# A hybrid attention and SSM layer on one core: SSM products of two halves in turn, joined scans, SSM issued ahead of the q and k pass, and row blocks in the order 0, 1, 3, 2

## The chip, the cores and the metric

The kernel runs on one core of a Trainium2 chip. The metric is device time in microseconds of one execution of the whole program, from inputs in HBM to outputs in HBM.

## The reference, cut to what matters

One layer over 2048 prompt rows and 64 sample rows of width 1024, in fp32:

```python
proj = x @ w_in                                  # q | k | v | u, 512 columns each
attn = diff_attention(rope(q), rope(k), v)       # 8 heads, two softmax maps each, chunk-causal
y    = Re(C h) + D u                             # S5 SSM: 32 groups of 16 channels, 64 complex states
ssm  = glu(gelu(y) @ w_glu + b_glu)
x1   = layer_norm(ALPHA * x + concat(attn, ssm) @ w_out)
x2   = layer_norm(ALPHA * x1 + square(relu(x1 @ w_up)) @ w_down)    # w_up 1024 x 4096
```

The sample rows attend to a cache of 1024 keys and values (`cache_k`, `cache_v`). The outputs are x2, the new k and v rows, and the last SSM states.

## The kernel before

**Products.** Most products are written as three fp32r products (`mm3`, L136 to L138): high times high, low times high, high times low. So each weight is split into a high part on ACT (L130) and a low part on DVE or POOL (L133). The SSM products are plain fp32, and each stands in the trace as two PE instructions.

**Stages.** (1) `proj_uv` makes u and v. (2) `proj_qk` makes q and k (PSUM tile `pm`), and beside it run `ssm_all` and `cache_keys`, which splits and stores the cached keys and values. (3) `attention` over 72 units (a unit is one head by 256 rows, or the 64 sample rows of one head; its product ends in the ACT copy `osb`, L581), beside it `glu` (`za`, `zb`) and then the row blocks. (4) What is left of the blocks.

**Row blocks.** Rows go through the last two lines of the reference in four blocks, three of 512 rows and block 3 of 576. `block_out` multiplies by w_out (`pd<-dh,bxh`), adds, takes the first layer norm (LN1) and transposes back (`pu<-ident,acc`, L1058). `block_ffn` goes over 32 slices f of w_up and w_down: the up product (`pu<-bxh,fwh`), relu squared (L1167), the down product (`pd<-dh,hh`); its `rest` is the last slices and the second layer norm (LN2). `blocks()` is a generator that `interleave` advances beside attention: blocks 0, 1 and 2 in it, block 3 in the code at the end, after attention's pools are closed.

**SSM.** `ssm_build` makes the matrices of 8 groups, `ssm_run` runs them, four times over. In `ssm_run`: input products (`psi`), a rotation (`turn`), 16 scans for the four pairs of groups in real and imaginary part (prompt of 256 steps and sample of 8 apart), the rotation back, and per group g the output: one product with `km` over 128 partitions and two with `gf` over 64, the even groups in partitions 0 to 63, the odd ones in 64 to 127, all three into one PSUM tile `psy` of the pool `ps`, which has two (PSB = 2). GELU then reads `psy` (ACT, DVE, ACT, DVE) and stores to `s_gy`, from which `glu` loads `gyg`.

**What sets the order.** The work is written as Python generators, and the Tile framework gives each engine one list of instructions in order; the priority of a stretch is set with `level(n)` (n times 100000), of attention with HIP = 200000. Within an engine nothing overtakes. All loads and stores are issued by one queue, SP's (L125). `U8` is the level of the SSM's steps beside the pass, 0 before. The weights of `glu` (`wrg`) have level U7 = 3. `cache_keys` has no level and one buffer for each of its tiles (CKB = 1).

Of the kernel before, what the change touches and what calls it, by code (L numbers as in the profile page):

```python
# [45 lines left out]
ZB = 1  # L46
# [10 lines left out]
R6 = 4  # L57
R7 = 0.75
LATE = 2
# [10 lines left out]
A0S = 0  # L70
U8 = 0
VVB = 2
# [41 lines left out]
def build(nc, tc, io, ctx):  # L114
# [556 lines left out]
    def ssm_disc(kp, sp):  # L671
# [74 lines left out]
    def ssm_build(w, bt):  # L746

        ss = k.ss  # L750
        HG = SSM_HG
# [44 lines left out]
        yield  # L796
        k0 = bp.tile([128, HG, 128], F32, tag="btm", name="k0")[0:C]
        dd = bp.tile([C, HG, C], F32, tag="dd", name="dd")
        for e in range(2):
            psk = pm.tile([C, HP, 128], F32, tag="pi", name="psk", bufs=IB)  # L800
            o = slice(e * 64, e * 64 + 64)
            for q in range(HP):
                for ri in range(2):
                    pe.matmul(psk[:, q, :], lhsT=bb[o, ri, q, :], rhs=m.gf[o, ri, q, 0:8, :].rearrange("p t c -> p (t c)"),
                              start=ri == 0, stop=ri == 1)
            act.activation(out=k0.rearrange("c (q e) n -> c e q n", e=2)[:, e], in_=psk, func=AF.Copy)
        tt(dve, dd, ss.dsb[:, gs].unsqueeze(2).to_broadcast([C, HG, C]), ident[0:C, 0:C].unsqueeze(1).to_broadcast([C, HG, C]), ALU.mult)
# [9 lines left out]
        for l in range(1, 8):  # L817
# [3 lines left out]
            for ri in range(2):  # L821
                tt(pool, e[:, ri, :, n:2 * n], e[:, ri, :, 0:n], ss.u[:, 0, l, qs].unsqueeze(2).to_broadcast([128, HP, n]), ALU.mult)
                tt(pool, tmp[:, ri], e[:, 1 - ri, :, 0:n], us, ALU.mult)
                tt(pool, e[:, ri, :, n:2 * n], e[:, ri, :, n:2 * n], tmp[:, ri], (ALU.subtract, ALU.add)[ri])
        pool.tensor_copy(out=e[:, :, :, JP:NJ], in_=e[:, :, :, 0:NJ - JP])
        w.mats = m
        yield

    def ssm_run(w, m, bt):
# [39 lines left out]
        for ri in range(2):  # L869
            for q in range(HP):  # L870
                for c0, c1, i in ((0, JP, 0.0), (JP + 1, NJ, h0[:, ri, q:q + 1])):
                    dve.tensor_tensor_scan(out=z[:, ri, q, c0:c1], data0=ss.rho[:, bt * HP + q:bt * HP + q + 1].to_broadcast([128, c1 - c0]),
                                           data1=v[:, ri, q, c0:c1], initial=i, op0=ALU.mult, op1=ALU.add)
        turn(v, z, (ALU.subtract, ALU.add))
        for i, j in enumerate((JP - 1, NJ - 1)):
            pool.tensor_copy(out=ss.fin[:, i, :, qs], in_=v[:, :, :, j])
        yield
        for g in range(HG):
            psy = pm.tile([128, 512], F32, tag="ps", name="psy")
            y = psy[:, :NJ]  # L880
# [5 lines left out]
            gy = sp.tile([128, NJ], F32, tag="gy", name="gy", bufs=GB)  # L886
            act.activation(out=gy, in_=y, func=AF.Square, scale=math.sqrt(0.044715))
            dve.scalar_tensor_tensor(out=gy, in0=gy, scalar=1.0, in1=y, op0=ALU.add, op1=ALU.mult)
            act.activation(out=gy, in_=gy, func=AF.Tanh, scale=GC)
            dve.scalar_tensor_tensor(out=gy, in0=gy, scalar=1.0, in1=y, op0=ALU.add, op1=ALU.mult)  # L890
            gg = bt * HG + g
            dma(out=GY[gg * C:(gg + 1) * C, :, :].rearrange("c t j -> t c j"), in_=gy)
            if g % 4 == 3:
                yield
# [396 lines left out]
    def blocks():  # L1291
        yield from urgent(fl, U4)
        block_pools(cw, w)
        for i, b in enumerate(B):
            b.px, b.h, b.hh, b.dd, b.loaded, b.early = w.x, w.h, w.h, w.dn, False, EARLY and i == 0
# [12 lines left out]
        for i in range(3):  # L1308
            b = B[i]
            if i and not b.loaded:  # L1310
                yield from rest()
                rest = none
                while not ready(b):
                    yield "wait"
                load(b)
            state.cur = i
            yield from block_out(w, b, rest)
            if i < 2:
                rest = yield from block_ffn(w, b, lambda: load_rows(B[i + 1]), lambda: load(B[i + 1]))
            else:  # L1320
                state.rest = yield from block_ffn(w, b)

# [26 lines left out]
    with cw:  # L1349
        f2 = blocks()  # L1350
        with ExitStack() as ca:
            a = attn_pools(ca, ABUF, APB)
            hd = [None]

            def main():
                hd[0] = yield from attention_all(a)
            interleave(main(), f2, None)
            for _ in hd[0]:
                next(f2, None)
            for _ in range(R5):  # L1360
                next(f2, None)
        with ExitStack() as c2:
            p = lambda n, b, **kw: c2.enter_context(tc.tile_pool(name="o" + n, bufs=b, side="right", **kw))
            b = B[3]
            while state.cur < 2:
                next(f2)
            b.px, b.pacc, b.h = p("x", 1), p("acc", 1), p("h", HB3)
            w.ps["pu"].append(p("pu", 2, space=PSUM))
            w.ps["pd"].append(p("pd", 3, space=PSUM))
            for _ in range(R6):  # L1370
                next(f2, None)
# [6 lines left out]
            def rest():
                yield from f2
                yield from state.rest()  # L1380
            interleave(block_out(w, b, rest), f2, R7)
            w.top.close()
            with ExitStack() as c3:
                b.hold, b.lg = HL, 1
                b.hh, b.dd = (c3.enter_context(tc.tile_pool(name="t" + n, bufs=i, side="left")) for n, i in (("h", HL), ("d", 2 * HL)))

                load_gb(b, "ln2", c3.enter_context(tc.tile_pool(name="tg", bufs=1, side="left")))

                def last():
                    r = yield from block_ffn(w, b)  # L1390
                    yield from r()
                run(last())

# [65 lines left out]
```

## Time and profile before

| | us |
|---|---|
| median of 3 runs | 3173.56 (3170.77 to 3175.68) |
| profiled execution, its time | 3174.97 |
| profiled execution, its span | 3173.1 |
| PE busy | 2909.3 (92%) |
| DVE, ACT, POOL busy | 1761.8, 1504.2, 1636.2 |
| mean granted clock of PE | 0.947 of full speed |

PE is the busiest engine, but a busy PE is not PE at its peak: a matmul that streams at half clock, or that waits for its input with the next one queued, counts as busy too. So the number of matmuls in a stretch is read beside the busy time. The chain that ended last is 55% PE, 12% DVE, 11% DMA.

### The profile page before, as it was taken

The page shows a single profiled execution, that of the slowest core. Times are in us where ns is not written, and L with a number is a line of the kernel's source. Part 1 is how long each engine was busy: PE and PEld are TensorE (multiplying, and loading weights), DVE is VectorE, ACT ScalarE, POOL GpSimd, SP SyncE. Part 2 cuts the span into 40 slices and gives each one's busy share as a digit, 9 for nine tenths or more (in the row PEclk, how much of TensorE's full clock was granted, in tenths as well). Part 3 has the DMA queues.
Part 4 walks back from the last instruction along what each step waited for, and adds up shares of the span by engine and source line. Part 5 has one row for each costly group of instructions (what it writes and reads, how often), then busy time and mean ns, then how long its engine had stood idle before and what let it go on. Part 6 is the DMA issues. An engine that isn't in the chain of part 4 may idle for free.

```text
span 3173.1 us, 46490 instructions
## 1 busy us (share of the span) xinstructions
PE 2909.3 (92%) x15648; PEld 2423.9 (76%) x15648; DVE 1761.8 (56%) x4631; ACT 1504.2 (47%) x2905; POOL 1636.2 (52%) x1552
## 2 busy tenths in 40 slices
PE   8999998998898999998689999986899998899996
PEld 7976666896687888786589888864777776788885
DVE  7126866677867665567876666654222226322225
ACT  3222223776775766665567766522232322332332
POOL 2236761455654666565546666534445544544443
PEclk9999998798899999998789999998899998899998
DMA  6368875658534444446434333265223322422221
GB/s 189 128 194 212 219 204 166 202 155 276 147 107 131 130 134 119 119 118 213 144 114 129 100 110 107 76 230 179 74 83 94 89 83 80 130 80 77 80 84 56
DMA packets 420195, 425.47 MB, mean 134 GB/s; under 512 B 53458, under 2 KB 313042, under 8 KB 418932
## 3 DMA queue, kind: packets, MB, share of 16 engines
q1 hardware_dynamic: 419956, 422.50, 45.0%
q8 instruction: 123, 2.02, 0.3%
q14 instruction: 116, 0.95, 0.1%
HBM read 328.76 MB, written 93.64 MB: 133 GB/s over the span
## 4 chain that ended last, share of the span: by engine, by line
PE 55%; DVE 12%; DMA 11%; POOL 6%; issue 4%; ACT 3%; SPq 1%; POOLq 0%; DVEq 0%; ACTq 0%
PE pd L136 7%; PE pd L137 7%; PE pd L138 7%; PE pu L136 5%; PE pu L138 5%; PE pu L137 5%; DMA raw<-in_w_up 4%; PE oT L575 4%; PE tps L559 3%; PE sps L512 3%; DMA raw<-in_w_down 2%; POOL dl L133 2%; POOL fwl L133 2%; DVE acc L141 2%; DMA raw<-in_ln_g 2%
## 5 line engine op out<-in xcount | busy, mean ns | idle before, releaser
L133 POOL TENSOR_TENSOR dl<-raw,dh 128x512 fp32r<-128x512 f32 x336 | 432.8, 1301 | 294.5 <-ACT dh L130 286.3
L133 POOL TENSOR_TENSOR fwl<-raw,fwh 128x512 fp32r<-128x512 f32 x256 | 332.3, 1300 | 380.2 <-ACT fwh L130 355.3
L136 PE MATMUL pu<-bxh,fwh 128*128 128x256 f32 (+2 forms) x1472 | 496.3, 339 | 26.0 <-ACT fr L1167 17.0
L515 DVE TENSOR_SCALAR_CACHE_REDUCE s<-sps 128x512 f32<-128x512 f32 (+5 forms) x688 | 402.9, 600 | 210.9 <-PE sps L512 132.3
L141 POOL TENSOR_TENSOR s<-s 128x512 f32<-128x512 f32 (+3 forms) x344 | 382.6, 1139 | 237.4 <-ACT s L543 237.0
L138 PE MATMUL pu<-bxh,fwl 128*128 128x256 f32 (+2 forms) x1472 | 491.4, 337 | 7.0 <-POOL fwl L133 6.1
L137 PE MATMUL pu<-bxl,fwh 128*128 128x256 f32 (+2 forms) x1472 | 490.6, 334 | 0.0
L136 PE MATMUL pd<-dh,hh 128*128 128x512 f32 (+1 forms) x1088 | 426.5, 400 | 18.6 <-DVE acc L141 10.1
L137 PE MATMUL pd<-dl,hh 128*128 128x512 f32 (+1 forms) x1088 | 430.8, 396 | 0.7 <-POOL dl L133 0.7
L141 DVE TENSOR_TENSOR acc<-acc,pd 128x512 f32<-128x512 f32 (+1 forms) x384 | 254.3, 682 | 302.1 <-PE pd L138 300.8
L523 ACT ACTIVATE s<-s,nm 128x1024 f32<-128x1024 f32 (+9 forms) x416 | 365.8, 881 | 116.7 <-DVE nm L520 113.0
L138 PE MATMUL pd<-dh,hl 128*128 128x512 f32 (+1 forms) x1088 | 419.5, 396 | 0.0
L130 ACT ACTIVATE dh<-raw 128x512 fp32r<-128x512 f32 x336 | 209.2, 628 | 353.8 <-PE pd L138 209.1
L130 ACT ACTIVATE fwh<-raw 128x512 fp32r<-128x512 f32 x256 | 160.5, 628 | 378.9 <-DMA raw<-in_w_up 243.0
L136 PEld LDWEIGHTS pu<-bxh,fwh 128*128 128x128 f32 x1472 | 283.7, 193 | 68.9 <-ACT fr L1167 28.5
L132 DVE CAST hh<-fr 128x256 fp32r<-128x256 f32 (+2 forms) x184 | 111.2, 604 | 397.3 <-ACT fr L1168 397.0
L138 PEld LDWEIGHTS pu<-bxh,fwl 128*128 128x128 f32 x1472 | 282.2, 193 | 40.7 <-POOL fwl L133 15.3
L137 PEld LDWEIGHTS pu<-bxl,fwh 128*128 128x128 f32 x1472 | 283.8, 193 | 26.4
L575 PE MATMUL oT<-w,vt 128*128 128x256 f32 (+3 forms) x1296 | 258.2, 301 | 18.2 <-DVE w L133 12.8
L136 PEld LDWEIGHTS pd<-dh,hh 128*128 128x128 f32 (+1 forms) x1088 | 202.0, 186 | 63.1 <-DVE acc L141 12.0
L575 PEld LDWEIGHTS oT<-w,vt 128*128 128x128 f32 (+1 forms) x1296 | 211.3, 202 | 48.1 <-DVE w L133 20.4
L512 PE MATMUL sps<-kst,qst 96*128 96x512 f32 (+2 forms) x544 | 218.6, 419 | 20.9 <-DVE s L515 18.5
(273 smaller groups left out, 5890.0 us busy)
## 6 DMA issues: line engine op xcount, KB each, us to landing
raw<-in_w_up SPq DMA_DIRECT2D x256, 256.0 KB
raw<-in_w_down SPq DMA_DIRECT2D x256, 256.0 KB
kst<-s_k SPq DMA_DIRECT2D x64, 384.0 KB
raw<-in_w_out SPq DMA_DIRECT2D x80, 256.0 KB
xr<-in_xT SPq DMA_DIRECT2D x64, 256.0 KB
vt<-s_v SPq DMA_DIRECT2D x32, 512.0 KB
qst<-s_q SPq DMA_DIRECT2D x64, 192.0 KB
raw<-in_ln_g SPq DMA_DIRECT2D x36, 256.0 KB
```

Source lines behind the costliest of these rows:

```text
L130: act.activation(out=dst_hi, in_=src, func=AF.Copy)
L132: hi_eng.tensor_copy(out=dst_hi, in_=src)
L133: (lo_eng or dve).tensor_tensor(out=dst_lo, in0=src, in1=dst_hi.bitcast(F32), op=ALU.subtract)
L136: pe.matmul(ps, lhsT=lh, rhs=rh, start=start, stop=False)
L137: pe.matmul(ps, lhsT=lh, rhs=rl, start=False, stop=False)
L138: pe.matmul(ps, lhsT=ll, rhs=rh, start=False, stop=stop)
L141: e.tensor_tensor(out=out, in0=a, in1=b, op=op)
L512: pe.matmul(ps[:nr, :e - c0], lhsT=qst[m][0:96, q], rhs=self.keys(m, 96, c0, e), start=True, stop=True)
L515: dve.tensor_scalar(out=s[:nr, o:o + c1 - c0], in0=ps[:nr, :c1 - c0], scalar1=1.0, scalar2=None, op0=ALU.mult, op1=ALU.max, accum_out=self ...
L523: act.activation(out=x, in_=x, func=AF.Exp, bias=nm, accum_out=self.ls[:nr, m, p:p + 1])
L559: pe.transpose(out=ps[:kr, i * nr:i * nr + nr], in_=self.s[t, 0, k_ * 128 // SC][:nr, o:o + kr], identity=ident[:nr, :nr])
L575: pe.matmul(self.oT[:, t * nr:(t + n) * nr], lhsT=vt[k_ // 8][:kr, k_ % 8, :], rhs=w[:kr, e, i * nr:(i + n) * nr], start=(k_ == 0 and e == ...
```

## The change

The SSM part: the `gf` products of an even and an odd group stand in turn, each of the pair with its own `psy` tile; the scans of one part are joined into one over 1060 steps, with a decay tile `rh` that holds zeros where a segment starts; the input products' copies are all on ACT; the products for `km` (`psk`) are done for both halves at once with a tile `bz` that holds `bb` in two blocks and zeros; and U8 = 1. The block part: `blocks()` ends with block 1; block 3 follows (`block_out` beside what is left of `f2`), then its FFN with block 2's `block_out` beside it, then block 2's FFN with block 3's `rest` beside it; both have their w_out weights in a pool of their own (`wo`).

```diff
-R7 = 0.75
+R7 = 1.0
+R8 = 0.4
-U8 = 0
+U8 = 1
...
+        m.rh = w.kp.tile([128, HP, NJ + 1], F32, tag="rh", name="rh", bufs=EB)
...
+        bz = bp.tile([128, 2, HP, 2, C], F32, tag="bz", name="bz")
+        pool.memset(bz, 0.0)
         for e in range(2):
-            psk = pm.tile([C, HP, 128], F32, tag="pi", name="psk", bufs=IB)
             o = slice(e * 64, e * 64 + 64)
-            for q in range(HP):
-                for ri in range(2):
-                    pe.matmul(psk[:, q, :], lhsT=bb[o, ri, q, :], rhs=m.gf[o, ri, q, 0:8, :].rearrange("p t c -> p (t c)"),
-                              start=ri == 0, stop=ri == 1)
+            pool.tensor_copy(out=bz[o, :, :, e, :], in_=bb[o])
+        psk = pm.tile([2 * C, HP, 128], F32, tag="pi", name="psk", bufs=IB)
+        for q in range(HP):
+            for ri in range(2):
+                pe.matmul(psk[:, q, :], lhsT=bz[:, ri, q].rearrange("p e c -> p (e c)"), rhs=m.gf[:, ri, q, 0:8, :].rearrange("p t c -> p (t c)"),
+                          start=ri == 0, stop=ri == 1)
...
+        pool.tensor_copy(out=m.rh, in_=ss.rho[:, qs].unsqueeze(2).to_broadcast([128, HP, NJ + 1]))
+        pool.memset(m.rh[:, :, 0:JP + 2:JP + 1], 0.0)
...
-                if ri == 0:
-                    act.activation(out=z[:, ri, q, :], in_=psi[:, :NJ], func=AF.Copy)
-                else:
-                    dve.tensor_copy(out=z[:, ri, q, :], in_=psi[:, :NJ])
+                act.activation(out=z[:, ri, q, :], in_=psi[:, :NJ], func=AF.Copy)
...
         for ri in range(2):
-            for q in range(HP):
-                for c0, c1, i in ((0, JP, 0.0), (JP + 1, NJ, h0[:, ri, q:q + 1])):
-                    dve.tensor_tensor_scan(out=z[:, ri, q, c0:c1], data0=ss.rho[:, bt * HP + q:bt * HP + q + 1].to_broadcast([128, c1 - c0]),
-                                           data1=v[:, ri, q, c0:c1], initial=i, op0=ALU.mult, op1=ALU.add)
+            dve.tensor_tensor_scan(out=zt[:, ri].rearrange("p q j -> p (q j)"), data0=m.rh.rearrange("p q j -> p (q j)"),
+                                   data1=vt[:, ri].rearrange("p q j -> p (q j)"), initial=0.0, op0=ALU.mult, op1=ALU.add)
...
-        for g in range(HG):
-            psy = pm.tile([128, 512], F32, tag="ps", name="psy")
-            y = psy[:, :NJ]
-            o = slice(g % 2 * 64, g % 2 * 64 + 64)
-            pe.matmul(y, lhsT=m.km[:, g, :], rhs=ug[:, g, :], start=True, stop=False)
+        for q in range(HP):
+            ys = [pm.tile([128, 512], F32, tag="ps", name="psy")[:, :NJ] for e in range(2)]
+            for e, y in enumerate(ys):
+                pe.matmul(y, lhsT=m.km[:, 2 * q + e, :], rhs=ug[:, 2 * q + e, :], start=True, stop=False)
             for ri in range(2):
-                pe.matmul(y, lhsT=m.gf[o, ri, g // 2, 1:9, :].rearrange("p t c -> p (t c)"), rhs=vt[o, ri, g // 2, 0:NJ], start=False, stop=ri == 1)
+                for e, y in enumerate(ys):
+                    o = slice(e * 64, e * 64 + 64)
+                    pe.matmul(y, lhsT=m.gf[o, ri, q, 1:9, :].rearrange("p t c -> p (t c)"), rhs=vt[o, ri, q, 0:NJ], start=False, stop=ri == 1)
...
-        for i in range(3):
+        for i in range(2):
...
+            b.hh = b.h
+            b.wo = l.wo = b.dd = p("wo", 4)
...
+            interleave(block_out(w, b, lambda: iter(())), f2, R7)
+            run(f2)
+            f3 = block_ffn(w, b)
...
+            interleave(main(), t, R8)
+            run(t)
+            l.hold, l.lg = HL, 1
...
+            interleave(got[0](), f4, 1.0)
```

In the last lines `b` is block 3, `l` block 2, `main` runs `f3`, `t` is block 2's loads and `block_out`, `f4` is block 2's FFN; the pools of its last slices are opened after that, and `run(f4)` ends the program.

**First place: PE, the SSM's output products near the end of the q and k pass.** `psy` is the PSUM tile of a group, `km` and `gf` its matrices, `ug` and `vt` the inputs. Before, one group after the other:

```order
L882 MATMUL psy_3645<-ug_3435,km_3080 128x265
L884 MATMUL psy_3645<-vt_3445,gf_3082 128x265 x2
L882 MATMUL psy_3655<-ug_3435,km_3080 128x265
L884 MATMUL psy_3655<-vt_3445,gf_3082 128x265 x2
L882 MATMUL psy_3665<-ug_3435,km_3080 128x265
L884 MATMUL psy_3665<-vt_3445,gf_3082 128x265 x2
```

Now, two tiles in turn:

```order
L888 MATMUL psy_3593<-ug_3387,km_3048 128x265
L888 MATMUL psy_3594<-ug_3387,km_3048 128x265
L892 MATMUL psy_3593<-vt_3397,gf_3050 128x265
L892 MATMUL psy_3594<-vt_3397,gf_3050 128x265
L892 MATMUL psy_3593<-vt_3397,gf_3050 128x265
L892 MATMUL psy_3594<-vt_3397,gf_3050 128x265
```

The two `gf` products of one group no longer follow each other; between them stands one of the other half. The last of them now stands before the pass's last transposes, while before six groups' products stood among attention's first ones.

**Second place: SP, the loads of GLU's weights (`wrg`).** `kst`, `qst` and `vt` are attention's loads, `s_kc` the stores of `cache_keys`. Before:

```order
L125 DMA kst<-s_k 96x512
L125 DMA kst<-s_km 3x512
L125 DMA qst<-s_q 96x512
L125 DMA wrg<-in_w_glu 128x1024 x2
L125 DMA gyg<-s_gy 128x2120
L125 DMA s_o<-o 128x2x64
```

Now:

```order
L126 DMA s_kc<-ckh 128x512
L126 DMA s_kc<-ckl 128x512
L126 DMA qst<-s_q 96x512
L126 DMA qst<-s_qm 3x512
L126 DMA kst<-s_k 96x1024
L126 DMA kst<-s_km 3x1024
L126 DMA wrg<-in_w_glu 128x1024 x2
L126 DMA vt<-s_v 128x1024
L126 DMA s_o<-o 128x2x64
```

The weights moved back in the queue, behind the last stores of `cache_keys` and behind loads of attention's second set of units; all of `cache_keys` now stands beside attention, on POOL and on SP. On PE the first GLU product stood behind 3 finished units, now behind 20.

**Third place: PE, block 2's LN1.** Before, the 32 transposes of block 2 stand in one row between its last w_out products and its first up products:

```order
L136 MATMUL pd<-dh,bxh 128x512
L137 MATMUL pd<-dl,bxh 128x512
L138 MATMUL pd<-dh,bxl 128x512
L1058 MATMUL pu<-ident,acc 128x128 x32
L136 MATMUL pu<-bxh,fwh 128x256
L137 MATMUL pu<-bxl,fwh 128x256
```

Now, four of block 2's transposes among block 3's FFN (down products of 64 rows are block 3's alone):

```order
L138 MATMUL pd<-dl,hh 128x512
L139 MATMUL pd<-dh,hl 64x512
L139 MATMUL pd<-dh,hl 128x512 x2
L1068 MATMUL pu<-ident,acc 128x128 x4
L139 MATMUL pu<-bxh,fwl 128x256
L137 MATMUL pu<-bxh,fwh 128x256
```

Block 2's LN1 has FFN products of another block on both sides. Block 3's w_out products and transposes stand behind the whole FFN of block 1, and its first up products follow directly.

## Rows read from the trace of the kernel before

**Rows 1.** Windows: length, busy us of PE, PEld, DVE, ACT, POOL (instructions), PEclk, DMA share, GB/s.

```profile
211.00:529.00 318.00, 297.98 (x1408) 213.59 (x1408) 226.56 (x349) 91.14 (x190) 191.54 (x295) 0.98 0.77 204
529.00:578.00 49.00, 34.93 (x106) 23.60 (x106) 24.40 (x110) 28.15 (x82) 11.86 (x16) 0.55 0.85 257
578.00:725.00 147.00, 142.97 (x1134) 140.48 (x1134) 110.67 (x413) 114.23 (x289) 78.25 (x99) 0.95 0.54 165
725.00:891.00 166.00, 140.17 (x697) 114.74 (x698) 136.65 (x433) 119.06 (x215) 103.85 (x89) 0.85 0.66 199
```

**Rows 2.** Windows of the blocks after attention's end.

```profile
2100.00:2200.00 100.00, 79.87 (x303) 58.67 (x301) 46.42 (x115) 21.64 (x31) 44.30 (x35) 0.93 0.71 239
2200.00:2250.00 50.00, 25.03 (x126) 20.87 (x126) 21.79 (x45) 14.57 (x23) 17.51 (x16) 0.63 0.23 67
2600.00:2650.00 50.00, 50.00 (x215) 38.06 (x214) 15.63 (x25) 10.72 (x17) 20.44 (x16) 1.00 0.24 72
2650.00:2700.00 50.00, 31.36 (x132) 23.75 (x130) 48.46 (x117) 16.28 (x22) 26.43 (x20) 0.77 0.25 75
2700.00:2750.00 50.00, 42.21 (x229) 37.13 (x230) 21.90 (x61) 14.25 (x26) 23.64 (x20) 0.85 0.51 157
2750.00:3100.00 350.00, 348.77 (x2031) 304.64 (x2030) 96.82 (x157) 110.11 (x215) 169.16 (x146) 1.00 0.28 82
```

**Rows 3.** Chain that ended last, at the loads after attention's end.

```profile
2100.69 12.38 DMA raw<-in_w_up
```

**Rows 4.** Timeline of PE, SSM output products: start us, us, instructions.

```profile
318.71 0.72 PE L884 MATMUL psy<-vt,gf 64*128 64x265 f32 x4 [1.30 <-DVE vt L141]
319.36 0.50 PE L137 MATMUL pm<-wl,xh 128*128 128x512 f32 x1
...
333.85 1.16 PE L884 MATMUL psy<-vt,gf 64*128 64x265 f32 x4
334.93 0.71 PE L882 MATMUL psy<-ug,km 128*128 128x265 f32 x2
```

**Rows 5.** Chain that ended last: the products for `km`.

```profile
248.73 6.11 PE psk L804 x31
```

**Rows 6.** Timeline of DVE: the scans of one pair of groups.

```profile
447.07 0.67 DVE L872 TENSOR_TENSOR_SCAN z<-rho,vt 128x256 f32<-128x256 f32 x1
447.67 0.20 DVE L872 TENSOR_TENSOR_SCAN z<-rho,h,vt 128x8 f32<-128x8 f32 x1
```

**Rows 7.** Timeline of ACT: ends of the first unit, the third and the 36th.

```profile
561.78 0.38 ACT L581 ACTIVATE osb<-oT 128x256 f32<-128x256 f32 x1 [0.80 <-PE oT L575]
...
574.33 0.36 ACT L581 ACTIVATE osb<-oT 128x256 f32<-128x256 f32 x1
...
1034.28 0.37 ACT L581 ACTIVATE osb<-oT 128x256 f32<-128x256 f32 x1
```

**Rows 8.** Tiles: min/median/max ns, first and last start; `cvv` and `s_kc` are `cache_keys`.

```profile
L514 PE MATMUL sps<-kst,qst x256: 222/283/582, 529.4 to 2014.9; 99*128 99x128 f32 x64, 99*128 99x256 f32 x64
L125 SPq DMA_DIRECT2D wrg<-in_w_glu x4: 351/362/422, 573.3 to 581.6; - x4
L133 POOL TENSOR_TENSOR cvv<-cvr,cvv x16: 724/740/4375, 218.7 to 317.5; 128x256 fp32r<-128x256 f32 x16
L125 SPq DMA_DIRECT2D s_kc<-ckh x16: 320/424/780, 325.8 to 439.7; - x16
```

**Rows 9.** Windows of `osb` on ACT: length, busy us (units ended).

```profile
725.00:891.00 166.00, 4.15 (x11) 0.85 0.66 199
```

**Rows 10.** Windows on PE to the 36th unit's end: `pu` (w_up), then `pd` (w_down).

```profile
891.00:1034.28 143.28, 58.19 (x388) 0.95 0.42 121
891.00:1034.28 143.28, 44.66 (x156) 0.95 0.42 121
```

**Rows 11.** Tile `gy`: GELU's steps, ns.

```profile
L887 ACT ACTIVATE gy<-psy x32: 370/393/395, 329.8 to 558.6; 128x265 f32<-128x265 f32 x32
L888 DVE SCALAR_TENSOR_TENSOR gy<-gy,psy x32: 416/432/434, 330.3 to 559.0; 128x265 f32<-128x265 f32 x32
```

More of the change, by code (lines that the diff above doesn't have):

```diff
@@ L733, in ssm_disc @@
         dma(out=KP[:, :, 0:112], in_=ss.zz.to_broadcast([C, G, 112]))
-        ss.dsb = kp.tile([C, G], F32, name="dsb")
+        ss.dsb = kp.tile([2 * C, G // 2], F32, name="dsb")
+        ss.id2 = kp.tile([2 * C, C], F32, name="id2")
+        tt(dve, ss.id2, ident[0:2 * C, 0:C], ident[0:2 * C, C:2 * C], ALU.add)
         dma(out=ss.dsb, in_=io["dT"])
@@ L796, in ssm_build @@
         yield
-        k0 = bp.tile([128, HG, 128], F32, tag="btm", name="k0")[0:C]
-        dd = bp.tile([C, HG, C], F32, tag="dd", name="dd")
+        k0 = bp.tile([128, HG, 128], F32, tag="btm", name="k0")[0:2 * C, 0:HP]
+        dd = bp.tile([2 * C, HP, C], F32, tag="dd", name="dd")
+        bz = bp.tile([128, 2, HP, 2, C], F32, tag="bz", name="bz")
+        pool.memset(bz, 0.0)
         for e in range(2):
-            psk = pm.tile([C, HP, 128], F32, tag="pi", name="psk", bufs=IB)
             o = slice(e * 64, e * 64 + 64)
-            for q in range(HP):
-                for ri in range(2):
-                    pe.matmul(psk[:, q, :], lhsT=bb[o, ri, q, :], rhs=m.gf[o, ri, q, 0:8, :].rearrange("p t c -> p (t c)"),
-                              start=ri == 0, stop=ri == 1)
-            act.activation(out=k0.rearrange("c (q e) n -> c e q n", e=2)[:, e], in_=psk, func=AF.Copy)
-        tt(dve, dd, ss.dsb[:, gs].unsqueeze(2).to_broadcast([C, HG, C]), ident[0:C, 0:C].unsqueeze(1).to_broadcast([C, HG, C]), ALU.mult)
+            pool.tensor_copy(out=bz[o, :, :, e, :], in_=bb[o])
[4 more added lines that the diff above has]
+                          start=ri == 0, stop=ri == 1)
+        act.activation(out=k0, in_=psk, func=AF.Copy)
+        tt(dve, dd, ss.dsb[:, qs].unsqueeze(2).to_broadcast([2 * C, HP, C]), ss.id2.unsqueeze(1).to_broadcast([2 * C, HP, C]), ALU.mult)
         tt(dve, k0[:, :, 0:C], k0[:, :, 0:C], dd, ALU.add)
-        dma(out=KP[:, gs, 112:240], in_=k0)
+        for e in range(2):
+            dma(out=KP.rearrange("c (q e) n -> e c q n", e=2)[e, :, qs, 112:240], in_=k0[e * C:e * C + C])
         for n in range(T):
@@ L838, in ssm_run @@
             dma(out=ug[(7 - s) * C:(8 - s) * C, :, :], in_=US.rearrange("(g c) s j -> s c g j", c=C)[s, :, gs, :])
-        z = bp.tile([128, 2, HP, NJ], F32, tag="z", name="z", bufs=ZB)
+        zt = bp.tile([128, 2, HP, NJ + 1], F32, tag="z", name="z", bufs=ZB)
+        z = zt[:, :, :, 1:NJ + 1]
         vt = bp.tile([128, 2, HP, NJ + 1], F32, tag="vt", name="vt")
@@ L877, in ssm_run @@
         yield
-        for g in range(HG):
-            psy = pm.tile([128, 512], F32, tag="ps", name="psy")
-            y = psy[:, :NJ]
-            o = slice(g % 2 * 64, g % 2 * 64 + 64)
-            pe.matmul(y, lhsT=m.km[:, g, :], rhs=ug[:, g, :], start=True, stop=False)
-            for ri in range(2):
-                pe.matmul(y, lhsT=m.gf[o, ri, g // 2, 1:9, :].rearrange("p t c -> p (t c)"), rhs=vt[o, ri, g // 2, 0:NJ], start=False, stop=ri == 1)
[L886 to L893, printed above, removed]
+        for q in range(HP):
+            ys = [pm.tile([128, 512], F32, tag="ps", name="psy")[:, :NJ] for e in range(2)]
+            for e, y in enumerate(ys):
+                pe.matmul(y, lhsT=m.km[:, 2 * q + e, :], rhs=ug[:, 2 * q + e, :], start=True, stop=False)
+            for ri in range(2):
+                for e, y in enumerate(ys):
+                    o = slice(e * 64, e * 64 + 64)
+                    pe.matmul(y, lhsT=m.gf[o, ri, q, 1:9, :].rearrange("p t c -> p (t c)"), rhs=vt[o, ri, q, 0:NJ], start=False, stop=ri == 1)
+            gs_ = [sp.tile([128, NJ], F32, tag="gy", name="gy", bufs=GB) for e in range(2)]
+            for y, gy in zip(ys, gs_):
+                act.activation(out=gy, in_=y, func=AF.Square, scale=math.sqrt(0.044715))
+                dve.scalar_tensor_tensor(out=gy, in0=gy, scalar=1.0, in1=y, op0=ALU.add, op1=ALU.mult)
+            for e, (y, gy) in enumerate(zip(ys, gs_)):
+                act.activation(out=gy, in_=gy, func=AF.Tanh, scale=GC)
+                dve.scalar_tensor_tensor(out=gy, in0=gy, scalar=1.0, in1=y, op0=ALU.add, op1=ALU.mult)
+                gg = bt * HG + 2 * q + e
+                dma(out=GY[gg * C:(gg + 1) * C, :, :].rearrange("c t j -> t c j"), in_=gy)
+            if q % 2:
                 yield
@@ L1294, in blocks @@
         for i, b in enumerate(B):
-            b.px, b.h, b.hh, b.dd, b.loaded, b.early = w.x, w.h, w.h, w.dn, False, EARLY and i == 0
+            b.wo, b.px, b.h, b.hh, b.dd, b.loaded, b.early = w.dn, w.x, w.h, w.h, w.dn, False, EARLY and i == 0
             b.eng1, b.eng2, b.lg, b.hold, b.gb, b.lg1, b.go = LNE, LNE2, LG2, 2, {}, LG, GO
@@ L1317, in blocks @@
             yield from block_out(w, b, rest)
[L1318 to L1321, printed above, removed]
+            rest = yield from block_ffn(w, b, *((lambda: load_rows(B[1]), lambda: load(B[1])) if i == 0 else ()))
+        yield from rest()
     def attention_all(a):
@@ L1359, in build @@
                 next(f2, None)
-            for _ in range(R5):
-                next(f2, None)
+        cps = cw.enter_context(ExitStack())
+        for t, n in (("pu", 2), ("pd", 3)):
+            w.ps[t].append(cps.enter_context(tc.tile_pool(name="o" + t, bufs=n, side="right", space=PSUM)))
         with ExitStack() as c2:
             p = lambda n, b, **kw: c2.enter_context(tc.tile_pool(name="o" + n, bufs=b, side="right", **kw))
-            b = B[3]
-            while state.cur < 2:
-                next(f2)
+            b, l = B[3], B[2]
             b.px, b.pacc, b.h = p("x", 1), p("acc", 1), p("h", HB3)
[L1368 to L1371, printed above, removed]
+            b.hh = b.h
+            b.wo = l.wo = b.dd = p("wo", 4)
             load_rows(b)
@@ L1374, in build, with third, main, last @@
             b.loaded = True
-            b.eng1, b.eng2, b.lg1, b.go = LNE3, LNE4, LG3, GO3
+            b.eng1, b.lg1, b.go = LNE3, LG3, GO3
             load_gb(b, "ln1", p("g", 1))
[L1378 to L1392, printed above, removed]
+            interleave(block_out(w, b, lambda: iter(())), f2, R7)
+            run(f2)
+            f3 = block_ffn(w, b)
+            def third():
+                load_rows(l)
+                load_mix(l, range(l.nt))
+                l.loaded = True
+                l.eng1, l.eng2, l.lg1, l.gb["ln1"] = LNE3, LNE4, LG3, b.gb["ln1"]
+                yield from block_out(w, l, lambda: iter(()))
+                yield "out"
+            got = []
+            def main():
+                got.append((yield from f3))
+            t = third()
+            interleave(main(), t, R8)
+            run(t)
+            l.hold, l.lg = HL, 1
+            got2 = []
+            def last():
+                got2.append((yield from block_ffn(w, l)))
+            f4 = last()
+            interleave(got[0](), f4, 1.0)
+        with ExitStack() as c3:
+            p = lambda n, b: c3.enter_context(tc.tile_pool(name="t" + n, bufs=b, side="right"))
+            l.hh, l.dd = p("h", HL), p("d", 2 * HL)
+            load_gb(l, "ln2", p("g", 1))
+            run(f4)
+            run(got2[0]())
+        w.top.close()
 _POS = np.concatenate([np.arange(SEQ).reshape(16, 16, 8).transpose(0, 2, 1).reshape(-1)])
```

4 lines of the change are left out of this document (2 added, 2 removed).

## The prediction

> **What bounds the kernel now.** I read the page's busy shares first, then windows by stage, then the chain and the rows at each edit. PE is busy for 2909 of 3173 us, so time can only be won where PE's products are made cheaper or where PE stands still. [Rows 1] show four stages. In the pass for q and k, 211 to 529 us, PE is busy 298 of 318 us and no other engine over 227: PE sets its length, and an SSM product made shorter there shortens the program. From 529 to 578 PE has 106 products in 49 us: attention's first units run almost alone, and the granted clock is 0.55. GLU then fills PE, 1134 products in 147 us, 0.130 us each. In the stage of block 0's w_out and LN1, 725 to 891, there are 697 products in 166 us, 0.238 each, and DVE is busy 137.
>
> After attention the loss is read from counts, since a waiting PE shows as busy. Products of 512 columns go at 0.233 us (215 in 50 us, the window at 2600), the mix of a whole FFN at 0.172 (2031 in 350 us) [rows 2]. At these rates 2100 to 2200 loses 100 − 303 × 0.233 = 29 us, where the chain waits 12.4 us for a load of w_up [rows 3]; 2200 to 2250, the turn of block 2's LN1, loses 35 (126 products, mostly of 256 columns and transposes, at about half of 0.233); 2650 to 2700, block 3's LN1 with DVE busy 48 of 50, loses 50 − 132 × 0.233 = 19; 2700 to 2750, its first slices, 50 − 229 × 0.172 = 10.5. Together about 94 us.
>
> **The SSM part.** The order of PE settles what the products do; the price is in [rows 4]. Four instructions of one half take 1.08 us (333.85 to 334.93). Where two groups happened to be side by side in opposite halves, four take 0.65 (318.71 to 319.36). So each of 32 groups saves 0.43 us, 13.8 in all, less the eighth that is in turn already: 12. The two `km` products of a pair stand side by side, with no row for a gain; I take 4, between 0 and 0.3 us for each group, 10. `psk` took 6.1 us for 31 instructions [rows 5], 0.197 each; 64 of 128 go: between 6 and 13 us, I take 8. Together 24 us of PE, bounds 15 to 35, in a stage that PE bounds.
>
> Scans: a scan of 256 columns takes 0.67 us and one of 8 0.20 [rows 6], so 1.9 ns a column and 0.19 at the start. A joined scan of 1060 is then about 2.2 us. Eight of them are 17.6 us against 32 × 0.87 = 28, so DVE is 10 us lighter. The input copies (16 of some 0.4) go to ACT, busy 91 of 318. POOL fills `rh` and `bz`, some 20 us by tiles of like size, and loses all of `cache_keys`. DVE, ACT and POOL stand below PE in this stage, so I put these at nothing. If PE fell by over 60 us, DVE would set the end; it does not. The first unit ends at 562 [rows 7], so now at about 538; the first attention product, which some 10 us of SSM products no longer follow, moves less, from 529 [rows 8] to 505 to 518.
>
> **What was moved behind it.** All of `cache_keys`, 16 steps, now stands beside attention, and on SP's queue the weights `wrg` stand behind its last stores. The order of PE puts GLU's first product behind 20 finished units instead of 3. Nothing overtakes on an engine, so 19 more units run with no other products on PE. They took 6.3 us each at 562 to 574 (two in 12.55 us [rows 7]). The other end is 166 / 11 = 15.1 us [rows 9], beside w_out, with DVE at 137 of 166; bare units are nearest to the first. I take 15 at 6.3 and 4, while the next loads come, at 10: 134 us. With 5 us from the weights' load at 573.3 [rows 8] to the first product at 578, GLU begins at 538 + 134 + 5 = 677. It then takes (768 + some 390 of attention) × 0.130 = 150 us, to about 828. With only 5.5 units beside it, block 0's w_out and LN1 have some 570 products × 0.238 = 136 us, to 964.
>
> The order places the 36th unit there. Before, that unit ended at 1034, but 544 FFN products of block 0 were done too: 103 us by their busy time [rows 10], and 82 at clear rates (388 × 0.117 + 156 × 0.233). I take 92. The early part thus stands at 964 + 92 − 1034 = **+22 us**, the 24 from the SSM counted in. If all 19 units go at 6.3, it is +7; its upper end is the first rival.
>
> **The blocks.** Block 2's LN1 now has block 3's FFN on both sides, so the 35 us of that turn go. Block 3's w_out and LN1 come right behind block 1's FFN, with no products beside them: the 19 us of LN1 and 10.5 of first slices are paid there instead. Block 3's loads come behind attention's end as block 2's did; I keep the 12.4 us of [rows 3] and drop the rest of the 29, since only one block is made ready at that point. Block 2's w_out and LN1 beside FFN cost products nothing but turns, 6 us, a third of an LN1. What remains is 19 + 10.5 + 12.4 + 6 = 48 of 94: **−46 us**. The bounds: if only the last 6 stays and two thirds of the rest is covered, −75; if the 29 and a second LN1 stay, −20. The program's end, the last LN2, has an FFN's weights loaded and the same work before it; I put it at nothing.
>
> **Sum:** +22 − 46 = −24 us against a span of 3173.1, so 3149, and with the 1.9 us around it (3174.97) **3151 us**; the median is 1.4 below that execution, which I leave inside the range.
>
> **A rule weighed.** The rows at 318.71 show two halves of PE's rows filling two PSUM tiles in 0.65 us instead of 1.08 [rows 4]. The Trainium skill, "TensorEngine Tiling (Array Packing)", section "Gotcha 1: PSUM Pressure", says that different row tiles write to different PSUM banks, cannot access one bank at the same time, and have to be synchronized by software. By that rule a pair takes both tiles of `ps`. The row agrees as far as two tiles go; that nothing is left to fill meanwhile is the third rival below.
>
> **Rivals.**
> *1. `cache_keys` holds GLU back (slower).* It has one buffer for each tile, and its loads and stores wait their turn on SP's queue. Beside the pass its 16 steps took from 218.7 to 439.7 [rows 8], 13.8 us each; if they keep that pace behind attention's start, they end at about 513 + 221 = 734, and GLU starts at 744. That is 67 later than 677, PE has nothing else in its list, and the time is 3151 + 67 = 3218. It decides from the point where GLU starts 22 us later than forecast, at 699 (a step of 11 us). Against it: beside the pass the steps were handed out by the pass's pace, and their POOL work is 0.74 us an instruction. For it: DMA was at 0.85 in the stage after 529 [rows 1].
> *2. The tail's wait only moves.* Block 3's loads, w_out and LN1 are bare, and block 2's LN1 stalls the FFN. Then the blocks give −20, and +22 − 20 = +2: 3177. For it: LN1 is bound by DVE at 48 of 50 [rows 2].
> *3. The pairs wait for GELU.* Both `psy` tiles are filled at once, so the next pair waits for ACT (0.39) and two DVE steps (0.43 each) [rows 11]: 1.25 us × 16 pairs = 20, and 3171. Against it, 20 to 28 products of the pass stand between pairs in PE's order, 4.7 to 6.5 us at 0.233. The pairs not running together at all would cost 12, less than this.
> *4. More gain.* Units go at 6.3 throughout (+7) and the tail gives 75: 3107.
>
> **How the numbers follow.** The forecast, 3125 to 3166: 0.47. More gain, 3090 to 3125: 0.15. No change by rival 2: 0.14, by rival 3: 0.04. Rival 1, 3181 to 3225: 0.20. Faster by over 0.2% (6.3 us, about what a measurement of this kernel can tell from no change) is 0.47 + 0.15 = 0.62, within it 0.18, slower 0.20. The range leaves out the ends of the first and the last case, 3105 to 3210. Both signs are open because a loss before 1000 us stands against a gain after 2050.
>
> **What would show it.** First unit's end at 530 to 545; four `gf` instructions in 0.65 us; GLU's first product at 660 to 700; block 0's first relu near 970; after attention, no window like that at 2200, but bare transposes of block 3 of some 20 us; and block 2's LN1 with PE at the FFN's rate. I am wrong if GLU starts behind 700, if more than 70 of the 94 us of loss remain, or if units alone take 8 us and more.

## The result: slower, and the profile after

| | before | changed |
|---|---|---|
| median, us | 3173.8 | 3198.1 (3194.8 to 3200.6) |
| ratio to before, 95% interval | | 1.0077, 1.0059 to 1.0094 |
| span of the profiled execution, us | 3173.1 | 3193.0 |

The change made the kernel slower by 0.8%, 24 us; the forecast was 3151. The windows of the changed kernel (columns as in [rows 1]: length, busy us of PE, PEld, DVE, ACT, POOL, PEclk, DMA share, GB/s) show where.

```profile
211.00:529.00 318.00, 292.43 (x1364) 213.96 (x1364) 213.63 (x268) 95.03 (x209) 183.47 (x283) 0.94 0.64 158
529.00:730.00 201.00, 144.37 (x558) 117.97 (x559) 136.84 (x572) 124.27 (x305) 81.41 (x95) 0.56 0.75 223
730.00:890.00 160.00, 156.45 (x1213) 151.13 (x1212) 116.52 (x374) 125.17 (x263) 93.63 (x108) 0.96 0.41 129
890.00:1040.00 150.00, 118.50 (x545) 90.69 (x543) 116.64 (x323) 90.87 (x176) 83.14 (x68) 0.84 0.65 202
```

The stage at a low granted clock was 49 us long in [rows 1] (clock 0.55) and is now 201 us long (0.56): attention's units alone, 558 products in 201 us, 0.36 us each, where GLU's stage behind it has 0.13. GLU itself takes 150 us, 3 more than before. The `osb` copies that end the first, the 20th and the 36th unit on ACT (start, us):

```profile
563.82 0.38 ACT L582 ACTIVATE osb<-oT 128x256 f32<-128x256 f32 x1 [0.35 <-PE oT L576]
...
726.90 0.36 ACT L582 ACTIVATE osb<-oT 128x256 f32<-128x256 f32 x1
...
1016.91 0.38 ACT L582 ACTIVATE osb<-oT 128x256 f32<-128x256 f32 x1 [1.34 <-PE sps L513]
```

The first unit ends no earlier than in [rows 7]. The 19 units behind it take 163 us, 8.6 each: the first 15 take 104 us, the last four 59. Tiles of the changed kernel, first and last start, answer to [rows 8]; the last is block 0's up product, the first of its FFN:

```profile
L126 SPq DMA_DIRECT2D s_gy<-gy x32: 575/590/1016, 321.6 to 550.7; - x32
L134 POOL TENSOR_TENSOR cvv<-cvr,cvv x16: 723/728/840, 569.8 to 630.1; 128x256 fp32r<-128x256 f32 x16
L126 SPq DMA_DIRECT2D s_kc<-ckl x8: 319/380/443, 644.2 to 718.5; - x8
L126 SPq DMA_DIRECT2D wrg<-in_w_glu x4: 333/342/432, 723.0 to 734.2; - x4
L137 PE MATMUL zb<-gh,whg x128: 276/281/562, 730.2 to 877.0; 128*128 128x256 f32 x112, 128*128 128x320 f32 x16
L137 PE MATMUL pu<-bxh,fwh x1472: 274/308/632, 1040.3 to 3154.3; 128*128 128x256 f32 x90, 128*128 128x512 f32 x72, 128*128 128x320 f32 x22
```

`cache_keys` begins only behind the SSM's last store of `gy` (550.7), runs from 570 to 719, the weights are loaded right behind it, and GLU's first product starts at 730.2. Beside the pass its first `cvv` stood at 218.7.

After attention the changed kernel gains. Its windows there answer to [rows 2]:

```profile
2100.00:2150.00 50.00, 46.38 (x195) 35.36 (x193) 10.92 (x17) 13.73 (x24) 24.44 (x19) 1.00 0.29 85
2200.00:2250.00 50.00, 45.07 (x190) 33.75 (x189) 33.35 (x94) 13.98 (x19) 23.76 (x18) 1.00 0.68 222
2250.00:2300.00 50.00, 37.90 (x138) 26.42 (x137) 28.33 (x75) 12.28 (x17) 24.08 (x19) 0.83 0.52 162
2300.00:2320.00 20.00, 12.00 (x52) 8.54 (x50) 18.40 (x22) 7.17 (x13) 15.44 (x10) 0.66 0.08 27
2400.00:2500.00 100.00, 96.51 (x516) 80.79 (x515) 53.68 (x95) 33.43 (x58) 52.10 (x41) 0.98 0.25 74
2500.00:2600.00 100.00, 100.00 (x593) 88.32 (x593) 28.19 (x47) 31.28 (x62) 47.29 (x41) 1.00 0.27 80
```

Block 3's bare w_out and LN1 end at 2320 (clock 0.83 and 0.66 from 2250 on, DVE busy 18 of the last 20 us). Block 2's LN1 lies in 2400 to 2500, with DVE twice as busy as in the next 100 us, and costs 77 products of 593, at 0.17 us some 13 us; the stall of 35 us of the kernel before is gone.

### The profile page after: what moved, and what is told of

It reads as the page before. It is cut to its first block, busy times and chain, and to the rows that moved or that the text cites. A ratio compares the mean times of both kernels' runs of the same rounds, so it can differ in the third digit from the quotient of the medians.

```text
span 3193.0 us, 46376 instructions
## 1 busy us (share of the span) xinstructions
PE 2934.3 (92%) x15584; PEld 2448.7 (77%) x15584; DVE 1746.7 (55%) x4560; ACT 1507.9 (47%) x2917; POOL 1664.6 (52%) x1572
## 4 chain that ended last, share of the span: by engine, by line
PE 61%; DMA 13%; DVE 12%; POOL 5%; issue 4%; ACT 3%; SPq 1%; DVEq 0%; POOLq 0%; ACTq 0%
PE pd L137 7%; PE pd L138 7%; PE pd L139 7%; PE pu L137 7%; PE pu L139 7%; PE pu L138 7%; PE oT L576 3%; PE tps L560 3%; PE sps L513 2%; DVE acc L142 2%; DMA raw<-in_w_up 2%; DMA raw<-in_ln_g 2%; DVE s L516 2%; SPq L126 1%; DMA raw<-in_w_down 1%
## 5 line engine op out<-in xcount | busy, mean ns | idle before, releaser
L134 POOL TENSOR_TENSOR dl<-raw,dh 128x512 fp32r<-128x512 f32 x336 | 440.1, 1322 | 305.3 <-ACT dh L131 284.4
L137 PE MATMUL pu<-bxh,fwh 128*128 128x256 f32 (+2 forms) x1472 | 489.4, 334 | 9.7 <-ACT fr L1177 6.6
L139 PE MATMUL pu<-bxh,fwl 128*128 128x256 f32 (+2 forms) x1472 | 483.3, 332 | 4.1 <-POOL fwl L134 3.5
L576 PE MATMUL oT<-w,vt 128*128 128x256 f32 (+3 forms) x1296 | 270.9, 311 | 19.0 <-DVE w L134 7.5
L513 PE MATMUL sps<-kst,qst 96*128 96x512 f32 (+2 forms) x544 | 230.9, 448 | 36.3 <-DVE s L516 34.1
```

Source lines behind the costliest of these rows:

```text
L134: (lo_eng or dve).tensor_tensor(out=dst_lo, in0=src, in1=dst_hi.bitcast(F32), op=ALU.subtract)
L137: pe.matmul(ps, lhsT=lh, rhs=rh, start=start, stop=False)
L139: pe.matmul(ps, lhsT=ll, rhs=rh, start=False, stop=stop)
L513: pe.matmul(ps[:nr, :e - c0], lhsT=qst[m][0:96, q], rhs=self.keys(m, 96, c0, e), start=True, stop=True)
L576: pe.matmul(self.oT[:, t * nr:(t + n) * nr], lhsT=vt[k_ // 8][:kr, k_ % 8, :], rhs=w[:kr, e, i * nr:(i + n) * nr], start=(k_ == 0 and e == ...
```

## The experiments

**The question.** What pushed `cache_keys` out of the pass? The edit of the SSM part nowhere names it. It makes the SSM's tiles larger, though: `rh` has 4256 bytes a partition, `bz` 1024. The Python code opens the buffers of `cache_keys` after it has closed those of the SSM, so the framework may give both the same bytes, and then the first user of the second has to wait for the last user of the first. The addresses in the built programs, bytes within a partition:

```
                    before            changed           fit
gy (two)            95936 to 98084    100992 to 103140  98752 to 100900
cvr, ckr            101280 to 103328  101280 to 103328  101280 to 103328
gl of GLU (first)   102496            102496            102496
```

In the changed kernel `gy`, from which the SSM's last stores go, lies on the first buffer of `cache_keys`; before there were 3196 bytes between them. GLU's `gl` lies on the buffers of `cache_keys` in all three, so by the addresses GLU follows `cache_keys` wherever that stands. Theory M: this overlap is the whole loss. Rival O: the products' new order and the level U8 = 1 cause it. Rival B: the block order causes it.

**fit: the same kernel, laid out closer.** The instructions are those of the changed kernel; their order on an engine is the framework's and comes out another way.

```diff
-        ss.zz = kp.tile([C, 1, 112], F32, name="zz")
+        ss.zz = sp.tile([C, 1, 112], F32, name="zz")
...
-        bb, t1 = (bp.tile(s3, F32, tag=n, name=n) for n in ("bb", "bt1"))
+        bb = bp.tile(s3, F32, tag="bb", name="bb")
+        t1 = bp.tile([128, HG, 128], F32, tag="btm", name="bt1")[:, 0].rearrange("p (r q c) -> p r q c", r=2, q=HP)
...
-        k0 = bp.tile([128, HG, 128], F32, tag="btm", name="k0")[0:2 * C, 0:HP]
-        dd = bp.tile([2 * C, HP, C], F32, tag="dd", name="dd")
-        bz = bp.tile([128, 2, HP, 2, C], F32, tag="bz", name="bz")
+        k0 = bp.tile([128, HG, 128], F32, tag="btm", name="k0")
+        dd = k0[0:2 * C, HP + 2, 0:HP * C].rearrange("p (q c) -> p q c", q=HP)
+        bz = k0[:, HP:HP + 2].rearrange("p a (q e c) -> p a q e c", q=HP, e=2)
+        k0 = k0[0:2 * C, 0:HP]
```

> The changed kernel with its SSM tiles laid closer: bz, dd and the scratch tile t1 live in the buffer of k0, zz moves to the set-up pool. The same instructions on the same data; only addresses change, so that the last gelu tile gy ends at byte 100928 of a partition, below cache_keys' first buffer at 101280 (in the changed kernel gy lies at 100992 to 103140, on top of it; in the kernel before it ended at 98084). Theory M (the shared bytes make cache_keys wait for the SSM's end, and GLU for cache_keys): cache_keys goes back beside the q and k pass, its first cvv before 330 us instead of 569, GLU's first product at 570 to 590 instead of 730, and about 3100 us in all (3080 to 3115): the loss of PE before 1040 us falls by some 110, the block part keeps its gain of about 63. Rival O (the new order of the SSM's products and level 1 of its steps push GLU back, not the addresses): GLU stays at 720 to 740 and the time within 10 us of 3198. Rival B (the block order is what costs): GLU may move, but the time stays above 3174.

Measured: 3123.7 us, ratio 0.9847 (0.9820 to 0.9874). Tiles of fit:

```profile
L134 POOL TENSOR_TENSOR cvv<-cvr,cvv x16: 725/738/1777, 220.6 to 317.7; 128x256 fp32r<-128x256 f32 x16
L126 SPq DMA_DIRECT2D wrg<-in_w_glu x4: 333/364/424, 582.3 to 592.2; - x4
L137 PE MATMUL zb<-gh,whg x128: 276/281/582, 587.9 to 731.2; 128*128 128x256 f32 x112, 128*128 128x320 f32 x16
```

`cache_keys` is back at 220.6 and GLU at 587.9. Rivals O and B fall; the time is 9 us above M's range, which had counted on some gain of the SSM part.

**before_pad: the kernel before, laid out wider.** Only the tile `et` gets 1264 unused floats at its end (`m.et = ...tile([128, 2 * HP * NJ + 1264]...)[:, 0:2 * HP * NJ]`).

> The kernel before with 5056 unused bytes at the end of the tile et, as many as the changed kernel's SSM tiles have grown; nothing else. Theory M: gy then lies on cache_keys' first buffer as in the changed kernel, cache_keys moves behind the SSM's end, GLU's first product from 578 to about 730, and the time rises by 85 to 115 us, to 3255 to 3290. Rival O and rival B: nothing but addresses changes, 3174 within 6.

Measured: 3258.5 us, ratio 1.0263 (1.0243 to 1.0282). The tiles of before_pad, and the window of the bare units:

```profile
L133 POOL TENSOR_TENSOR cvv<-cvr,cvv x16: 723/727/732, 553.6 to 620.6; 128x256 fp32r<-128x256 f32 x16
L125 SPq DMA_DIRECT2D wrg<-in_w_glu x4: 333/357/971, 710.2 to 723.5; - x4
L136 PE MATMUL zb<-gh,whg x128: 276/281/550, 717.5 to 872.6; 128*128 128x256 f32 x112, 128*128 128x320 f32 x16
```

```profile
564.00:717.00 153.00, 122.62 (x481) 100.57 (x481) 112.75 (x465) 100.76 (x245) 70.20 (x80) 0.56 0.70 212
```

Unused bytes alone cost 84 us against the 3174.6 beside it, with the same late GLU and the same clock of 0.56. That is the price of the overlap, measured without a single instruction of the change.

**blocks_only and ssm_only: one half of the change each**, the functions of the other half as before (U8, and the layout of the input `dT`, go with the SSM half).

> The kernel before with the block part of the change alone (blocks 0, 1, 3, 2, R7, R8, pools wo), SSM as before. Theory M: GLU at 578 as before, the tail gains what the two profiles show behind attention's end (loss of PE 187 before, 124 after): 3110, between 3095 and 3128. Rival B: the block order costs, 3180 or more. Rival O: as theory M, 3095 to 3128.

> The kernel before with the SSM part alone (products in turn, joined scans, km for both halves, U8 = 1), blocks as before. Theory M: GLU's first product at about 730, and 3174 + 85, between 3240 and 3275. Rival O: the same. Rival B: within 10 us of 3174.

Measured: 3123.5 (0.9831, 0.9808 to 0.9855) and 3256.4 (1.0257, 1.0234 to 1.0280). The block order gains 51 us; the SSM half loses 82, and before_pad loses as much with no SSM edit. And fit, which has both halves without the overlap, is no faster than blocks_only: the SSM half as it stands in fit is worth nothing measurable. That is not yet a price of the products in turn: in the lists on PE, the second `gf` product follows the first of its own tile in 24 of 32 groups before, in 2 in the changed kernel, and in 18 in fit, so fit has lost most of the turns. No run shows what the 30 turns of the changed kernel are worth without the overlap. The next eight runs ask about the other pieces.

**The SSM half, piece by piece, in fit.** Theory P: the SSM's own chain over DVE and POOL paces the pass. Rival E: PE does. fit_pe: every `psk` product three times over. fit_level0: U8 = 0. fit_oldscan: 64 scans with a start value in place of `rh`. fit_rh_act: the copies into `rh` by `act.activation` in place of `pool.tensor_copy`.

> The compact kernel (label fit) with every product for km (psk) done three times over, so PE gets back some 16 us of work (128 more instructions at 0.125 us in fit's trace) in the pass for q and k. Theory P (with the SSM part the pass is paced by the SSM's own chain through DVE, POOL and loads, and PE has room: 286 of 318 us busy against 302 in blocks_only): 3124 to 3130, at most 6 above fit's 3123.7. Rival E (PE still sets the pass): 3136 to 3142, as many us longer as PE got.

> The compact kernel (fit) with U8 = 0 instead of 1: the SSM's steps get no level ahead of the pass. Theory P: within 8 of fit's 3123.7, since the chain has the same steps either way. Rival L (it is the level that loses what the products save, because PE's list then has SSM products whose inputs are late in front of the pass's ready ones): 3105 to 3115.

> The compact kernel (fit) with the scans of the kernel before (64 scans with a start value, no rh, no copies for it on POOL). Joined scans save DVE 28 - 19 = 9 us and cost POOL four copies of 2.75 us. Theory P, the chain on DVE paces the pass: 3126 to 3134, up to 9 us longer. If the copies on POOL cost as much as the scans save: within 3 of 3123.7. Rival E: within 3 as well.

> The compact kernel (fit) with the copies into rh on ACT (busy 90 of 318 us in the pass) instead of POOL (202 of 318). Theory P with POOL in the chain: 5 to 12 us shorter, 3112 to 3119. If POOL's copies lie beside other work: within 4 of 3123.7.

scan_level0 joins the scans of before and U8 = 0; scan_level0_seq also writes the output products one group after the other.

> The compact kernel with both of the last two gains: the scans of the kernel before and U8 = 0. What is left of the SSM part: products in turn in the source, km for both halves, copies on ACT. If old scans (-17) and level 0 (-10) act in different places: 3094 to 3100. If both remove the same wait: 3103 to 3110.

> As scan_level0, with the output products and GELU one group after the other, as in the kernel before. In the compact kernel's list on PE 18 of 32 second products follow the first of their own tile all the same (2 in the changed kernel, 24 in the kernel before), so the turn is worth little here: within 5 of scan_level0. Rival E (every us of PE in the pass counts, 0.43 us for each group): 6 to 13 longer.

| run | us | ratio, 95% interval | first unit's end |
|---|---|---|---|
| blocks_only | 3123.5 | 0.9831 (0.9808 to 0.9855) | 564.7 |
| fit | 3123.7 | 0.9847 (0.9820 to 0.9874) | 574.3 |
| fit_pe | 3134.6 | 0.9872 (0.9852 to 0.9891) | 593.7 |
| fit_level0 | 3113.5 | 0.9806 (0.9783 to 0.9829) | 565.2 |
| fit_oldscan | 3106.5 | 0.9787 (0.9765 to 0.9809) | 569.0 |
| fit_rh_act | 3120.2 | 0.9829 (0.9810 to 0.9849) | 578.1 |
| scan_level0 | 3115.2 | 0.9819 (0.9795 to 0.9842) | 565.7 |
| scan_level0_seq | 3111.7 | 0.9807 (0.9784 to 0.9829) | 570.1 |
| fit_et | 3104.7 | 0.9770 (0.9757 to 0.9784) | 570.0 |
| oldscan_et | 3123.9 | 0.9825 (0.9805 to 0.9846) | 562.5 |

The ratios are good to 4 to 9 us either way, so a difference of two of them has to be over 10 us or so to count. fit_pe is longer than fit by 11 us in the medians, which had different runs of the kernel before beside them, and by 8 in the ratios: it lies between both models, and the time settles neither. Its first unit ends 19 us later for 16 us of PE, so the products still stand in the chain there. But what the change takes off PE does not bring the first unit forward either: it ends at 562 to 578 in every other kernel. fit_level0, 10 us below fit, is in rival L's range, at the edge of what can be told apart. fit_rh_act is 3.5 us below fit, no difference. fit_oldscan, which I expected the same or slower, is 17 us faster, clear of the noise: in this layout the joined scans with their copies cost time. The two do not add: 3115 with both, where the sum of both gains would be 3097. Between scan_level0 and scan_level0_seq there is no measurable difference, as expected from the list on PE.

**A held engine.** One loss inside the pass is seen in the changed kernel. Its timelines of DVE, of POOL and of PE near 323 us:

```profile
323.07 13.47 DVE L134 TENSOR_TENSOR xl<-xr,xh 128x512 fp32r<-128x512 f32 x1 [2.39 <-ACT xh L131]
336.46 1.02 DVE L868 COPY z<-h 128x8 f32<-128x8 f32 x1
```

```profile
323.55 0.32 POOL L142 TENSOR_TENSOR et<-et,etm 128x64 f32<-128x64 f32 x1
...
329.65 1.06 POOL L142 TENSOR_TENSOR et<-et,uu 128x512 f32<-128x512 f32 x1
...
333.66 2.33 POOL L142 TENSOR_TENSOR et<-et,etm 128x512 f32<-128x512 f32 x2
336.07 1.39 POOL L142 TENSOR_TENSOR btm<-bb,pg 128x512 f32<-128x512 f32 x1
```

```profile
338.80 2.14 PE L888 MATMUL psy<-ug,km 128*128 128x265 f32 x4 [6.67 <-DVE gy L900]
```

A subtract whose median is 0.69 us takes 13.47. It starts 0.5 us before a run of `et` on POOL, 19 products in a row without a gap, and ends at 336.54, just behind that run. GELU's DVE steps stand behind it, and PE waits 6.67 us for them. fit has the same picture near its pass's end: 6.13 us on DVE, up to the end of POOL's run at 494.48. An earlier copy of 8 columns with one input stands 7.38 us there, and again ends with POOL's last `et` product (360.77).

```profile
353.43 7.38 DVE L870 COPY z<-h 128x8 f32<-128x8 f32 x1
...
488.64 6.13 DVE L134 TENSOR_TENSOR xl<-xr,xh 128x256 fp32r<-128x256 f32 x1 [0.81 <-ACT xh L131]
```

```profile
359.59 1.18 POOL L142 TENSOR_TENSOR et<-et,etm 128x512 f32<-128x512 f32 x1
...
492.17 2.31 POOL L142 TENSOR_TENSOR et<-et,etm 128x512 f32<-128x512 f32 x2
```

Summed over the DVE instructions of the pass that are over 2 us longer than the median of their tile: 4.2 us before, 2.3 in blocks_only, 16.7 in the changed kernel, 12.0 in fit, 5.8 in fit_oldscan. before_pad, which has no edit of the SSM, has 12.9, so the holding does not need the change's instructions. The Trainium skill, "SBUF — State Buffer", section "SBUF: two separate sides", says that a GpSimd instruction that reads SBUF and a VectorE one with two SBUF inputs take a shared port pair by an exclusive lock, for a whole instruction, and the other fully blocks. The rows of the two subtracts agree that it blocks, and show it longer than one instruction: in the first through all 19.

fit_et and oldscan_et move the last doubling of `et` to DVE (`eng = dve if l == 7 else pool` for its three products), in fit and in fit_oldscan.

> The compact kernel (fit) with the last doubling of et (six products of 512 elements for each of four batches) on DVE instead of POOL: POOL 26 us less, DVE some 17 us more in the pass. Theory S (DVE products stand still while POOL issues its et products without a break: in the changed kernel one subtract xl of 0.69 us takes 13.47 us, 323.07 to 336.54, and ends when POOL's run of et ends; in fit one takes 6.13): the longest such run goes, DVE products held over 2 us past their median fall from 12.0 us to below 6 in the pass, the first unit ends 5 to 12 us before fit's 574, and the time is 3112 to 3120. Rival D (DVE's load is what counts, the holding lies beside other work): 3124 to 3135.

> The same move of et's last doubling in fit_oldscan (3106.5), where DVE products were held for 5.8 us in all. Theory S: little to gain, 3102 to 3110. Rival D: 3107 to 3118.

The held time fell from 12.0 to 3.4 us in fit_et, as it should if POOL's run is what holds DVE. The first unit ends 4.4 us earlier, just short of the 5 expected, but the time falls by 19, more than the pass gave. Nor does held time alone set the time: fit_rh_act had 28.9 us of it and was no slower than fit. In oldscan_et the first unit is 6.5 us earlier and the time 17 us longer in the medians, 12 in the ratios. That is against theory S; rival D's range ends 6 us below it, within the noise. In the profiled executions of fit_oldscan and oldscan_et the last `zb` product of GLU starts at 727.8 and 721.8, and the spans are 3101.6 and 3128.3 us (the latter the slowest of its five): 33 us are lost behind GLU, where the edit changed no instruction. So the difference of two such kernels is not set in the pass alone. The framework orders everything behind an edit anew; that these orders differ by some 15 us either way is how I read it, not shown. I did not find which later wait it is, and the worth of the single SSM pieces stays open.

## Why the prediction was wrong, step by step

- **What it forecast.** 3151, with a chance of 0.62 for faster. The sign was wrong: the blocks' term was right, the early term was not.
- **"Together 24 us of PE ... in a stage that PE bounds": failed.** The saving on PE is there. Windows of `psy` and of `psk` on PE, first of the kernel before, then of the changed one:

```profile
211.00:560.00 349.00, 57.28 (x192) 0.94 0.77 205
211.00:560.00 349.00, 15.79 (x128) 0.94 0.77 205
```

```profile
211.00:560.00 349.00, 45.71 (x192) 0.91 0.66 167
211.00:560.00 349.00, 10.29 (x64) 0.91 0.66 167
```

  11.6 and 5.5, together 17 of the 24. (All 128 `psk` products took 15.79 us, 0.123 each and not 0.197, and a quarter of the groups was in turn before, not an eighth.) It bought nothing: the first unit was to end at 538 and ended at 563.8, against 561.8. The pass itself ended no earlier. Its products `pm`, before and in the changed kernel:

```profile
L138 PE MATMUL pm<-wh,xl x272: 387/389/795, 212.9 to 523.4; 128*128 128x512 f32 x136
```

```profile
L139 PE MATMUL pm<-wh,xl x272: 387/389/796, 212.1 to 525.1; 128*128 128x512 f32 x136
```

  Behind it PE stood still twice on the way to the first unit, for a load and for a split on DVE that itself waited 5.80 us for a store:

```profile
543.95 0.45 PE L515 MATMUL sps<-kst,qst 99*128 99x128 f32 x1 [8.27 <-DMA kst<-s_k]
...
560.77 0.87 PE L560 MATMUL tps<-ident,s 128*128 128x128 f32 x3 [9.18 <-DVE tpl L134]
```

```profile
557.05 0.69 DVE L134 TENSOR_TENSOR tpl<-pt,tph 128x512 fp32r<-128x512 f32 x1 [5.80 <-DMA s_q<-tpl]
```

  Those 17 us are waits for loads and stores; in the kernel before, PE did the SSM's last groups in that time. So PE busy 298 of 318 us did not mean that work taken off PE shortens the way to the first unit. I put DVE's and POOL's share of it at nothing by their busy time, and did not price the loads and stores behind the pass at all.
- **"134 us" for 19 bare units: mis-sized, 163.** I took 15 at 6.3 us and four at 10; the 15 took 6.9 each, the four 14.9. Together with the 26 us above GLU began at 730 instead of 677. GLU's own 150 us were right (730 to 880). Block 0's w_out and LN1, put at 136, took 160 (880 to the first up product at 1040), so the point forecast for 964 came at 1040.
- **The sum of the early part, +22: mis-sized.** ssm_only measures it at +82, before_pad at +84 for the overlap alone.
- **Rival 1 was what happened**, at a chance of 0.20: GLU held behind `cache_keys`, decisive from 699, measured 730; its price was 3218, the time 3198. I had the place from the order of SP and PE, and read it as a change of order. I never asked why `cache_keys` had moved, and so took the 20 units for the whole of it. With the steps at 9 us instead of 13.8 the last store went out at 719, and GLU's first weights behind it were loaded and converted at 730 (`whg` on ACT, 729.02 to 730.07), just as PE was through with the 20 units.
- **"The blocks, −46": right.** blocks_only: −51. The place was right too: bare LN1 of block 3, none at block 2's turn.
- **Rival 3** (the pairs wait for GELU, 20 us) was met in part: PE's waits for GELU's `gy` in the pass are 8.0 us in all in the changed kernel, none in the kernel before, but 6.7 of them come from the held DVE above, not from the pairs. Another 4.7 us are put down to a store of `gy`.

## What to carry to other kernels

A tile that grows can move work that the edit never touches: where two pools share bytes, the later one waits for the earlier one's last user, so look at addresses when a stretch of work leaves its place in the order, and test it with padding. Keep the block order and give the SSM the room: fit_et, at 3104.7 us (0.9770, 0.9757 to 0.9784), beats both kernels. And count an engine as the bound of a stage only when taking work off it was seen to shorten the stage; busy share alone did not tell it here.

## What was not expected of the hardware

A DVE subtract of 0.69 us stood for 13.47 us beside 19 POOL products without a gap between them, a second of 0.42 us for 6.13, and a copy of 8 columns for 7.38; all three ended with POOL's run. Putting the copies into `rh` on ACT, which took work from POOL, did not lessen this: the DVE instructions of that pass were held for 28.9 us instead of 12.0.
